# Feed-forward down projection of a two-layer decoder trunk: weight block B11 stays in SBUF for two block sums, every second f tile's four parts share one 8 KB buffer, and the low parts of u go to VectorE in the four products with a block sum

## The chip, the cores and the metric

The kernel runs on one core of a Trainium2 chip, as one program. The metric is the device time of one execution in microseconds (us), as the median of several runs.

## The reference

Two layers are applied to x[1, 1024, 1024] in float32. Layer 0 mixes tokens with forgetting attention and latent attention side by side, layer 1 with differential attention; behind each mixer stands a feed-forward part with a causal depthwise convolution. The change lies in the feed-forward part alone, in its last product.

```python
def _conv_ffn(h, w_up, conv_w, conv_b, w_down):
    gate, val = jnp.split(h @ w_up, [D_FF], axis=-1)          # D_FF = 2816
    act = jax.nn.gelu(_causal_dwconv(gate, conv_w, conv_b), approximate=True)
    return (act * val) @ w_down
...
    for layer in range(DEPTH):                                # DEPTH = 2
...
        x = x + _rms_norm(m, norm_mix_post[layer])
        h = _rms_norm(x, norm_ffn_pre[layer])
        f = _conv_ffn(h, ffn_w_up[layer], ffn_conv_w[layer], ffn_conv_b[layer], ffn_w_down[layer])
        x = x + _rms_norm(f, norm_ffn_post[layer])
```

## The kernel before

**Exact products from split operands.** TensorE (PE) multiplies float32r operands, which carry fewer bits than float32. So each operand is split: `split` (L120) copies the leading bits to `hi` on ScalarE (ACT, line L122 in the trace) and subtracts them from the raw value to get `lo` on the engine given to it (L123). A product is three matmuls: hi·hi, hi·lo and lo·hi (`hl`, `mm3`, L143).

**The down projection (`ffn_down`, once in each layer).** u = act · val is 1024 tokens x 2816 features, W_down 2816 x 1024. Both are cut into 2 x 2 blocks: u into A11 ... A22 (token half, f half), W_down into B11 ... B22 (f half, column half). Strassen's scheme in Winograd's form needs seven block products in place of eight, with sums of blocks as operands. Sums of u (S1 to S4) were made by the up projection and lie in DRAM (`u_d`, in the trace uS; plain blocks uA). Sums of weights are made here on VectorE (DVE) by `comb` (L675), f tile by f tile: T3 = B22 - B12, T2 = T3 + B11, T1 = B12 - B11, T4 = B21 - T2. T3 and then T2 stay in three 8 KB buffers `t3q` (dT in the trace), so that T4 can use T2.

The products run on PE strictly one after another: A11·B11, A12·B21, S3·T3, S2·T2, S1·T1, S4·B22, A22·T4. Each has 11 f tiles (NP = 11, taken in pairs by the loop over `g0`), and an f tile 4 token tiles x 3 = 12 matmuls of 128 x 512, so that a product has 132. Four PSUM banks hold a product's result, and products alternate between two sets of four (`sa`, `sb_`). Between products their results are added up in the tiles C (`q1`, `c11`, `q7`, `c22`), mostly on DVE. `fin_e` and `fin_a` start the norm of finished rows (`post_early`, L200 on POOL; `post_late`, L209 to L213), `fin_b` transposes the next layer's normed rows on PE (layer 0 only). The last product keeps its last 5 f tiles (`TAIL`) back and then does them token tile by token tile.

**What a pair of f tiles takes.** One SyncE (SP) load of u (`uraw`, two buffers of pool `raw`); a load of weights through `bload` (L669; `wdraw`, six 4 KB buffers of pool T) or, for a sum, two for T3 and T1 and one for T2 and T4, then `comb`; per f tile two `split` calls into four buffers `d` (ah, al, bh, bl) of 2 KB from pool Q, which has 18, that is room for four and a half f tiles. The lo parts of u go to GpSimd (POOL), those of the weights to DVE; only in the first pair of A11·B11 both go to POOL. B11 is loaded three times in a layer: for A11·B11, T2 and T1. The pool X has fourteen 8 KB buffers; here it holds dT (3), C (4), and the rows of the norm (`xq`).

**What sets the order.** The code gives the instructions in program order; the framework's scheduler then orders each engine's list by its own model of the durations, and pools hand out buffers in that order. At run time every engine takes its list strictly in order, waiting on semaphores. So the order is fixed at build time, and an instruction that waits holds up all that stand behind it on its engine. SP issues the loads in such a list too.

Of the kernel before, what the change touches and what calls it, by code (L numbers as in the profile page):

```python
# [14 lines left out]
AF = mybir.ActivationFunctionType  # L15
# [32 lines left out]
# columns of the packed per-partition vectors  # L48
C_CW = 0            # [layer][tap][f]
C_CB = 132          # [layer][f]  # L50
# [12 lines left out]
def trunk(ctx: ExitStack, tc: tile.TileContext, a: dict):  # L63
# [36 lines left out]
    # the table that has Sqrt, before there is anything to take a root of  # L100
    warm = sb.tile([P, 1], F32, tag="warm", name="warm")
    nc.scalar.activation(warm, epsc, AF.Sqrt)
    # the tensor engine's clock rises after some microseconds of work: products that nobody reads, while the
    # first loads are on their way
# [15 lines left out]
    def split(raw, hi, lo, lo_eng=nc.gpsimd):  # L120
        """hi + lo == raw exactly: hi keeps the leading bits that a float32r product takes, lo the rest"""
        nc.scalar.copy(R(hi), raw)  # L122
        lo_eng.tensor_tensor(R(lo), raw, hi, ALU.subtract)  # L123

    def wload(src, n, tag="WL", cw=HALF, lo_eng=nc.gpsimd):
        """n columns per partition of weights -> [(hi, lo)] in chunks of cw columns"""
# [27 lines left out]
    def rstd_col(ss, scale, which):  # L154
        """(ss * scale + eps) ** -0.5 of one column, refined once"""
# [8 lines left out]
    def rstd_newton(ss, scale, out, eps=None):  # L164
        """(ss * scale + eps) ** -0.5 without the Sqrt table: a seed from the exponent bits, three Newton steps"""
# [20 lines left out]
    def xq_pair(tag):  # L186
        """two [tok, d] tiles: the residual's rows, the normalised ones"""
# [8 lines left out]
    def post_early(n, src, g_post, junk):  # L196
        """for a column half that is there before the other: its squares' sum, then times the gain (in place)"""
# [5 lines left out]
    def post_late(m, n, src, sse, early, g_post, xi, xq, pool, cut=False):  # L203
        """x[xi + 1][m] = x[xi][m] + norm(rows) * g_post; column half n last, the other from post_early"""
# [12 lines left out]
    def pre_norm_a(xq, g):  # L217
        """xr [tok, d] -> normalised rows"""
# [6 lines left out]
    def pre_norm_b(xq, evac):  # L225
        """normalised rows, transposed; evac(kg, bank) takes [d in 4 tiles, tok]"""
# [20 lines left out]
    def hk(hT, half, k, ts=slice(0, HALF)):  # L247
        """(hi, lo) of feature tile k, a token half"""
        return tuple(hT[half, k // 4, j][:, k % 4, ts] for j in range(2))

    def projT(w, hT, half, nk=KT, M=P, tag="mm"):
        """(W^T h^T)[M, half of the tokens]; w: chunks of 4 feature tiles"""
# [9 lines left out]
    # Other products fill the tensor engine beside attention. They are generators that yield after a few  # L262
# [1059 lines left out]
```

## Time and profile before

| | us |
|---|---|
| median of three runs | 2642.51 (2638.03, 2642.51, 2645.48) |
| profiled execution, span | 2644.6 |
| its PE busy | 2482.9 (94%) |
| layer 0, the seven products | 1098.4 to 1339.0 |
| layer 1, the seven products | 2391.1 to 2632.8 |

For the profiled execution the trace gives its span, 2644.6 us, and no other time; the span is inside the spread of the three runs. Times in the trace are counted from the start of the span. A row of the timeline reads: start, duration, engine, line, operation, out<-in, shape, count of instructions grouped in the row, and in brackets the idle time of the engine ahead of it with what ended that idle time. A row of windows gives the stretch, its length, the busy time of PE, PEld (weight load), DVE, ACT and POOL with their instruction counts, then TensorE's granted clock (1.00 is 2.4 GHz, 0.50 is 1.2 GHz), the share of the DMA engines' time and GB/s. The down projection is 241 us of the span in layer 0 and 242 us in layer 1; the rest (attention, up projections) is not touched by the change.

### The profile page before, as it was taken

The page shows a single profiled execution, that of the slowest core. Times are in us where ns is not written, and L with a number is a line of the kernel's source. Part 1 is how long each engine was busy: PE and PEld are TensorE (multiplying, and loading weights), DVE is VectorE, ACT ScalarE, POOL GpSimd, SP SyncE. Part 2 cuts the span into 40 slices and gives each one's busy share as a digit, 9 for nine tenths or more (in the row PEclk, how much of TensorE's full clock was granted, in tenths as well). Part 3 has the DMA queues.
Part 4 walks back from the last instruction along what each step waited for, and adds up shares of the span by engine and source line. Part 5 has one row for each costly group of instructions (what it writes and reads, how often), then busy time and mean ns, then how long its engine had stood idle before and what let it go on. Part 6 is the DMA issues. An engine that isn't in the chain of part 4 may idle for free.

```text
span 2644.6 us, 36732 instructions
## 1 busy us (share of the span) xinstructions
PE 2482.9 (94%) x12326; PEld 2077.6 (79%) x12326; DVE 1831.6 (69%) x3539; ACT 1235.4 (47%) x2463; POOL 1451.3 (55%) x1264
## 2 busy tenths in 40 slices
PE   9999899997899999989989999999969999999897
PEld 7878788786688888777778888978757888887685
DVE  5555788658866676576876776776787656665758
ACT  4455578655333333344545555555443333334343
POOL 2445665436787767656521323232278776766575
PEclk9999999899899999999999999999989999999999
DMA  3332323334132222575531212133522232226764
GB/s 138 91 90 77 117 78 92 101 107 160 52 113 107 106 99 107 192 247 196 199 136 57 64 53 82 59 96 104 167 88 83 105 112 99 107 109 219 254 218 149
DMA packets 177597, 319.31 MB, mean 121 GB/s; under 512 B 17256, under 2 KB 68088, under 8 KB 177408
## 3 DMA queue, kind: packets, MB, share of 16 engines
q1 hardware_dynamic: 177408, 316.97, 35.9%
q8 instruction: 97, 1.59, 0.2%
q14 instruction: 92, 0.75, 0.1%
HBM read 225.37 MB, written 76.85 MB: 114 GB/s over the span
## 4 chain that ended last, share of the span: by engine, by line
PE 56%; DVE 13%; DMA 5%; issue 3%; POOL 2%; ACT 2%; SPq 0%; POOLq 0%; DVEq 0%; ACTq 0%
PE psmm L143 26%; PE pstr L143 10%; PE psS L143 9%; PE pspv L143 8%; DMA wdraw<-in_ffn_down_dram 3%; DVE d L123 2%; PE pstr L370 1%; DVE xn L223 1%; DVE wdraw L675 1%; POOL d L123 1%; DVE dT L675 1%; DMA uraw<-uA 1%; DVE t L339 1%; DVE xq L211 1%; PE pstr L1133 0%
## 5 line engine op out<-in xcount | busy, mean ns | idle before, releaser
L123 POOL TENSOR_TENSOR d<-uraw,d 128x512 fp32r<-128x512 f32 x154 | 237.5, 1559 | 150.2 <-ACT d L122 130.2
L143 PE MATMUL psmm<-hT,whi 128*128 128x512 f32 (+1 forms) x960 | 310.5, 400 | 0.3 <-DVE qb L311 0.3
L123 POOL TENSOR_TENSOR wlo<-wraw,whi 128x512 fp32r<-128x512 f32 (+2 forms) x96 | 128.4, 1345 | 261.0 <-ACT whi L122 249.5
L347 ACT ACTIVATE t<-t,mn 128x896 f32<-128x896 f32 (+7 forms) x256 | 198.9, 778 | 124.5 <-DVE mn L339 116.0
L143 PEld LDWEIGHTS psmm<-hT,whi 128*128 128x128 f32 (+1 forms) x960 | 175.5, 190 | 33.9 <-PE pstr L1152 0.4
L143 PE MATMUL psmm<-hT,wlo 128*128 128x512 f32 (+1 forms) x480 | 189.7, 396 | 0.0
L143 PE MATMUL psS<-d,d 128*128 128x512 f32 x528 | 149.9, 410 | 31.9 <-DVE d L123 23.2
L123 DVE TENSOR_TENSOR d<-wdraw,d 128x512 fp32r<-128x512 f32 x106 | 130.9, 1260 | 65.6 <-ACT d L122 58.7
L122 ACT CAST d<-uraw 128x512 fp32r<-128x512 f32 x154 | 95.0, 617 | 172.4 <-DMA uraw<-uS 73.0
L597 DVE TENSOR_TENSOR u<-u,psmm 128x512 f32<-128x512 f32 x44 | 30.2, 687 | 190.6 <-PE psmm L143 166.7
L143 PEld LDWEIGHTS psS<-d,d 128*128 128x128 f32 x528 | 100.2, 195 | 64.5 <-DVE d L123 33.8
L143 PE MATMUL psmm<-wo,ot 128*128 128x512 f32 x576 | 147.7, 397 | 0.0
L143 PE MATMUL pstr<-d,d 128*128 128x512 f32 x594 | 147.6, 392 | 0.0
L370 PE MATMUL pstr<-ident,t 128*128 128x128 f32 x864 | 136.7, 280 | 7.4 <-POOL t L887 1.7
L143 PE MATMUL psmm<-d,d 128*128 128x512 f32 x462 | 135.5, 396 | 6.5 <-DVE d L123 6.4
L143 PEld LDWEIGHTS pstr<-d,d 128*128 128x128 f32 x594 | 112.6, 190 | 23.9
L608 ACT ACTIVATE y<-y,cols 128x1024 f32<-128x1024 f32 x44 | 50.7, 1153 | 170.4 <-DVE y L606 170.4
L143 PE MATMUL psmm<-whi,hT 128*128 128x256 f32 (+1 forms) x576 | 123.4, 300 | 3.0 <-DVE qb L311 1.6
L143 PEld LDWEIGHTS psmm<-wo,ot 128*128 128x128 f32 x576 | 105.8, 189 | 20.8 <-DVE qb L311 0.2
L370 PEld LDWEIGHTS pstr<-ident,t 128*128 128x128 f32 x864 | 103.2, 145 | 16.7 <-POOL t L887 3.5
L375 DVE TENSOR_TENSOR ptq<-pstr,ptq 128x512 fp32r<-128x512 f32 (+1 forms) x160 | 99.4, 630 | 22.2 <-ACT ptq L374 18.1
L143 PE MATMUL psmm<-T,S2h 128*128 128x512 f32 x352 | 110.2, 393 | 4.8 <-DVE T L123 4.8
(342 smaller groups left out, 7491.5 us busy)
## 6 DMA issues: line engine op xcount, KB each, us to landing
wdraw<-in_ffn_down_dram SPq DMA_DIRECT2D x90, 512.0 KB, 4.9
wg<-in_ffn_up_dram SPq DMA_DIRECT2D x44, 512.0 KB, 3.4
wv<-in_ffn_up_dram SPq DMA_DIRECT2D x44, 512.0 KB, 3.4
uS<-us SPq DMA_DIRECT2D x88, 256.0 KB, 2.0
uraw<-uS SPq DMA_DIRECT2D x40, 512.0 KB, 4.8
uA<-y SPq DMA_DIRECT2D x66, 256.0 KB, 2.1
ot<-oT SPq DMA_DIRECT2D x64, 256.0 KB, 3.4
uraw<-uA SPq DMA_DIRECT2D x30, 512.0 KB, 4.1
```

The lines of the kernel that those rows point to most:

```text
L122: nc.scalar.copy(R(hi), raw)
L123: lo_eng.tensor_tensor(R(lo), raw, hi, ALU.subtract)
L143: ins = nc.tensor.matmul(out, R(l), R(r), start=first and j == 0, stop=last and j == n - 1).ins
L211: nc.vector.scalar_tensor_tensor(xn[:, cs], src, r, g_post[:, cs], ALU.mult, ALU.mult)
L223: nc.vector.scalar_tensor_tensor(xn, xr, r, g, ALU.mult, ALU.mult)
L339: nc.vector.tensor_tensor_reduce(t[:, d0:d1], sp[:, d0 - c0:d1 - c0], bb[:, d0:d1], scale, BIG if mn is None else mn, ALU.add, ALU.min, m2)
L347: nc.scalar.activation(t[:, :W], t[:, :W], AF.Exp, bias=mn, scale=-1.0, accum_out=l)
L370: nc.tensor.transpose(tp[:, c:c + P], pts[qi][:, b * P:(b + 1) * P], ident)
L375: nc.vector.tensor_tensor(R(pl[:, :c]), tp[:, :c], ph[:, :c], ALU.subtract)
L597: nc.vector.tensor_tensor(u2, s1, p6, ALU.add)
L608: nc.scalar.activation(y, y, AF.Gelu_apprx_tanh, bias=cb)
L675: nc.vector.tensor_tensor(d, xx, yy, op)
```

## The change

The diff also drops comments and docstrings, which moves line numbers; left out below. What it does, all in `ffn_down`:

- Three more X buffers, `b11q` (dB in the trace), take B11 directly from DRAM, in six loads per layer. A11·B11 splits from them, and `comb` for T2 and T1 reads them. The twelve loads of B11 for T2 and T1 in each layer are gone (54 weight loads per layer become 42), and B11 takes no T buffer.
- With `wide`, the second f tile of each pair has its four parts in one X buffer ([P, 4, 512], 8 KB) in place of four Q buffers. It is on in all products of layer 1 and in the first five of layer 0. The last f tile of the last product keeps its two T buffers.
- In the products with T1, T2, T3 and T4 the lo parts of u are subtracted on DVE and no longer on POOL: 44 instructions in each layer, 88 in all.
- One ACT instruction (`warm`, a square root of a constant column) stands at the head of `ffn_down`.

```diff
         wd = a["ffn_down"][layer]
-        t3q = [buf("X", "dT") for _ in range(3)]
+        b11q, t3q = ([buf("X", n) for _ in range(3)] for n in ("dB", "dT"))
         t3 = lambda g: t3q[g // 4][:, g % 4, :]
+        b11 = lambda g: b11q[g // 4][:, g % 4, :]
+
+        nc.scalar.activation(warm, epsc, AF.Sqrt)
...
         def btiles(name, g, n):
+            t, b0 = ([f(g + i) for i in range(n)] for f in (t3, b11))
+            if name == "B11":
+                nc.sync.dma_start(b11q[g // 4][:, g % 4:g % 4 + n, :], wd[g:g + n, :, :HALF].rearrange("g p c -> p g c"))
+                return b0
             if name[0] == "B":
                 return bload(int(name[1]) - 1, int(name[2]) - 1, g, n)
-            t = [t3(g + i) for i in range(n)]
             if name == "T1":
                 b = bload(0, 1, g, n)
-                return comb(b, b, bload(0, 0, g, n), ALU.subtract)
+                return comb(b, b, b0, ALU.subtract)
             if name == "T3":
                 return comb(t, bload(1, 1, g, n), bload(0, 1, g, n), ALU.subtract)
             if name == "T2":
-                return comb(t, t, bload(0, 0, g, n), ALU.add)
+                return comb(t, t, b0, ALU.add)
...
-        def prod(an, bn, tags, between=(), tail=0):
+        def prod(an, bn, tags, between=(), tail=0, wide=True):
...
                         ah, al, bh, bl = t = tuple(x[:, c * HALF:(c + 1) * HALF] for x in (buf("T", "d"), buf("T", "d")) for c in range(2))
+                    elif i and wide:
+                        dq = buf("X", "d")
+                        ah, al, bh, bl = t = tuple(dq[:, c, :] for c in range(4))
                     else:
                         ah, al, bh, bl = t = tuple(buf("Q", "d") for _ in range(4))
-                    split(ar[:, i * HALF:(i + 1) * HALF], ah, al, nc.gpsimd)
+                    split(ar[:, i * HALF:(i + 1) * HALF], ah, al, nc.vector if bn[0] == "T" else nc.gpsimd)
...
-        p = prod("S4", "B22", sb_)
+        p = prod("S4", "B22", sb_, wide=layer == 1)
...
-        p = prod("A22", "T4", sa, [lambda t=t: fin_b(t) for t in range(4)], TAIL)
+        p = prod("A22", "T4", sa, [lambda t=t: fin_b(t) for t in range(4)], TAIL, layer == 1)
```

Where the instructions now stand is shown at three places. First, DVE in layer 0 at the start of S3·T3. Before (L739 adds A12·B21's banks to C and so waits for that product's end on PE; `dT<-dT,wdraw` is T2's sum, `d<-dT,d` a lo part of the weights of S3·T3):

```order
L739 TENSOR_TENSOR C2686_11318<-C2685_11317,psmm2749_11576 128x512
L739 TENSOR_TENSOR C2686_11318<-C2685_11317,pstr2750_11577 128x512
L675 TENSOR_TENSOR dT2682_11314<-dT2682_11314,wdraw2888_12125 128x512 x2
L739 TENSOR_TENSOR C2686_11318<-C2685_11317,pstr2751_11578 128x512
L739 TENSOR_TENSOR C2686_11318<-C2685_11317,pstr2752_11579 128x512
L675 TENSOR_TENSOR dT2682_11314<-dT2682_11314,wdraw2898_12171 128x512
L123 TENSOR_TENSOR d2842_11927<-dT2682_11314,d2841_11926 128x512
L675 TENSOR_TENSOR dT2682_11314<-dT2682_11314,wdraw2898_12171 128x512
L123 TENSOR_TENSOR d2849_11955<-dT2683_11315,d2848_11954 128x512
L675 TENSOR_TENSOR dT2683_11315<-dT2683_11315,wdraw2908_12217 128x512
L123 TENSOR_TENSOR d2853_11975<-dT2683_11315,d2852_11974 128x512
L675 TENSOR_TENSOR dT2683_11315<-dT2683_11315,wdraw2908_12217 128x512
```

And in the changed kernel, the twelve rows that end with the lo parts of f tile 4 of S3·T3, `d2808` from u and `d2810` from T3 (`wdraw<-wdraw,dB` is T1's sum, for the product after next; x2 means two instructions; the first of the four L748, the old L739, stands fourteen rows above the first row here):

```order
L678 TENSOR_TENSOR dT2685_11317<-dT2685_11317,dB2682_11314 128x512
L678 TENSOR_TENSOR wdraw2893_12404<-wdraw2893_12404,dB2683_11315 128x512 x2
L678 TENSOR_TENSOR wdraw2900_12447<-wdraw2900_12447,dB2683_11315 128x512 x2
L678 TENSOR_TENSOR dT2685_11317<-dT2685_11317,dB2682_11314 128x512
L678 TENSOR_TENSOR wdraw2907_12490<-wdraw2907_12490,dB2684_11316 128x512 x2
L678 TENSOR_TENSOR dT2685_11317<-dT2685_11317,dB2682_11314 128x512
L678 TENSOR_TENSOR wdraw2914_12533<-wdraw2914_12533,dB2684_11316 128x512
L678 TENSOR_TENSOR dT2686_11318<-dT2686_11318,dB2683_11315 128x512
L123 TENSOR_TENSOR d2808_11915<-uraw2804_11906,d2807_11914 128x512
L123 TENSOR_TENSOR d2811_11934<-uraw2804_11906,d2811_11934 128x512
L123 TENSOR_TENSOR d2819_11979<-dT2686_11318,d2819_11979 128x512
L123 TENSOR_TENSOR d2810_11917<-dT2686_11318,d2809_11916 128x512
```

Between the first L748 and the lo parts of f tile 4 stand all of T1's sums, and lo parts of u, where before T2's sums and lo parts of the weights took turns.

Second, SP at the same place of layer 0. Before (L669 weights, L706 u; wdraw2888 to wdraw2938 are B11 for T2):

```order
L669 DMA wdraw2878_12092<-in_ffn_down_dram 128x512
L669 DMA wdraw2888_12125<-in_ffn_down_dram 128x2x512
L669 DMA wdraw2898_12171<-in_ffn_down_dram 128x2x512
L706 DMA uraw2843_11944<-uS30_107 128x2x512
L669 DMA wdraw2908_12217<-in_ffn_down_dram 128x2x512
L669 DMA wdraw2918_12263<-in_ffn_down_dram 128x2x512
L669 DMA wdraw2928_12309<-in_ffn_down_dram 128x2x512
L669 DMA wdraw2938_12355<-in_ffn_down_dram 128x512
L706 DMA uraw2854_11992<-uS30_107 128x2x512
L669 DMA wdraw2948_12392<-in_ffn_down_dram 128x2x512
```

In the changed kernel (L672 weights, L712 u; wdraw2879 to wdraw2914 are B12 for T1; uraw2804 is the third pair of S3·T3):

```order
L672 DMA wdraw2829_12043<-in_ffn_down_dram 128x512
L712 DMA uraw2796_11861<-uS30_107 128x2x512
L672 DMA wdraw2830_12045<-in_ffn_down_dram 128x512
L672 DMA wdraw2879_12318<-in_ffn_down_dram 128x2x512
L672 DMA wdraw2886_12361<-in_ffn_down_dram 128x2x512
L672 DMA wdraw2893_12404<-in_ffn_down_dram 128x2x512
L672 DMA wdraw2900_12447<-in_ffn_down_dram 128x2x512
L672 DMA wdraw2907_12490<-in_ffn_down_dram 128x2x512
L672 DMA wdraw2914_12533<-in_ffn_down_dram 128x512
L712 DMA uraw2804_11906<-uS30_107 128x2x512
```

The six loads ahead of a u load were T2's and are now T1's; they stand ahead of the third pair's u, where before they stood ahead of the fourth's (uraw2854).

Third, DVE in layer 1's last product, A22·T4. Before (L211 and L213 are the norm of rows that S4·B22 finished; `d<-wdraw,d` is a lo part of T4; the last of them is `d6151`):

```order
L213 SCALAR_TENSOR_TENSOR xq6083_25658<-C5687_24027,rrpost6086_25664,xq6083_25658 128x512
L211 SCALAR_TENSOR_TENSOR xq6088_25677<-C5686_24026,rrpost6091_25683,gains5682_24021 128x512
L213 SCALAR_TENSOR_TENSOR xq6088_25677<-C5687_24027,rrpost6091_25683,xq6088_25677 128x512
L161 SCALAR_TENSOR_TENSOR rrpost6096_25702<-cvpost6095_25701,rrpost6096_25702 128x1
L123 TENSOR_TENSOR d6131_25839<-wdraw6123_25812,d6130_25838 128x512
L123 TENSOR_TENSOR d6137_25865<-wdraw6133_25858,d6136_25864 128x512
L211 SCALAR_TENSOR_TENSOR xq6093_25696<-C5686_24026,rrpost6096_25702,gains5682_24021 128x512
L213 SCALAR_TENSOR_TENSOR xq6093_25696<-C5687_24027,rrpost6096_25702,xq6093_25696 128x512
L123 TENSOR_TENSOR d6141_25873<-wdraw6133_25858,d6140_25872 128x512
L123 TENSOR_TENSOR d6147_25887<-wdraw6143_25880,d6146_25886 128x512
L123 TENSOR_TENSOR d6155_25906<-wdraw6153_25902,d6155_25906 128x512
L123 TENSOR_TENSOR d6151_25895<-wdraw6143_25880,d6150_25894 128x512
```

In the changed kernel (`d5945` is the product's last lo part):

```order
L123 TENSOR_TENSOR d5944_25673<-uraw5942_25668,d5944_25673 128x512
L160 SCALAR_TENSOR_TENSOR cvpost5890_25446<-rrpost5891_25447,cvpost5890_25446 128x1
L159 RECIPROCAL rrpost5901_25485<-cspost5902_25486 128x1
L160 SCALAR_TENSOR_TENSOR cvpost5895_25465<-rrpost5896_25466,cvpost5895_25465 128x1
L161 SCALAR_TENSOR_TENSOR rrpost5886_25428<-cvpost5885_25427,rrpost5886_25428 128x1
L123 TENSOR_TENSOR d5945_25674<-wdraw5943_25670,d5945_25674 128x512
L161 SCALAR_TENSOR_TENSOR rrpost5891_25447<-cvpost5890_25446,rrpost5891_25447 128x1
L160 SCALAR_TENSOR_TENSOR cvpost5900_25484<-rrpost5901_25485,cvpost5900_25484 128x1
L161 SCALAR_TENSOR_TENSOR rrpost5896_25466<-cvpost5895_25465,rrpost5896_25466 128x1
L211 SCALAR_TENSOR_TENSOR xq5883_25422<-C5599_23929,rrpost5886_25428,gains5592_23920 128x512
L213 SCALAR_TENSOR_TENSOR xq5883_25422<-C5600_23930,rrpost5886_25428,xq5883_25422 128x512
L211 SCALAR_TENSOR_TENSOR xq5888_25441<-C5599_23929,rrpost5891_25447,gains5592_23920 128x512
```

All lo parts of the product now stand ahead of the four pairs of L211 and L213, which before stood among them.

## Rows read from the trace of the kernel before

**Rows 1.** The page's first part: busy time, share and instructions of each engine.

```profile
PE 2482.9 (94%) x12326; PEld 2077.6 (79%) x12326; DVE 1831.6 (69%) x3539; ACT 1235.4 (47%) x2463; POOL 1451.3 (55%) x1264
```

**Rows 2.** Windows of layer 0's products, without the sixth (columns as told above).

```profile
1098.40:1131.90 33.50, 31.41 (x133) 24.50 (x134) 21.26 (x15) 14.07 (x25) 27.81 (x18) 1.00 0.78 274
1131.90:1163.30 31.40, 30.20 (x133) 24.59 (x132) 18.51 (x19) 14.31 (x26) 16.80 (x12) 1.00 0.74 250
1163.30:1204.60 41.30, 33.73 (x134) 26.33 (x133) 35.07 (x35) 14.61 (x30) 24.07 (x16) 0.92 0.70 248
1204.60:1235.80 31.20, 30.22 (x134) 24.64 (x133) 16.11 (x18) 15.92 (x29) 19.12 (x13) 1.00 0.53 179
1235.80:1265.70 29.90, 29.90 (x133) 24.76 (x132) 19.53 (x19) 13.34 (x24) 22.71 (x15) 1.00 0.58 200
...
1296.00:1339.00 43.00, 36.55 (x159) 28.22 (x158) 40.33 (x85) 25.27 (x56) 16.44 (x10) 0.96 0.46 157
```

**Rows 3.** Windows of layer 1's products, without the fifth and sixth.

```profile
2391.10:2427.80 36.70, 34.58 (x132) 26.70 (x133) 20.91 (x15) 14.10 (x25) 27.68 (x18) 0.91 0.74 251
2427.80:2459.30 31.50, 30.35 (x134) 24.73 (x133) 18.90 (x19) 14.31 (x26) 16.89 (x12) 1.00 0.73 248
2459.30:2499.60 40.30, 33.75 (x133) 25.17 (x132) 33.46 (x35) 13.68 (x29) 22.31 (x15) 0.96 0.70 251
2499.60:2535.10 35.50, 32.40 (x133) 25.75 (x133) 16.65 (x19) 16.91 (x31) 20.43 (x15) 0.95 0.50 161
...
2595.00:2632.80 37.80, 32.27 (x133) 25.49 (x131) 32.88 (x58) 16.07 (x37) 22.62 (x14) 0.95 0.28 94
```

**Rows 4.** Timeline of PE where it waits in the products.

```profile
1098.37 0.73 PE L143 MATMUL psS<-d,d 128*128 128x512 f32 x2 [1.33 <-ACT d L122]
...
1179.15 2.50 PE L143 MATMUL psS<-d,d 128*128 128x512 f32 x5 [5.03 <-DVE d L123]
...
1324.48 1.09 PE L231 MATMUL pstr<-ident,xq 128*128 128x128 f32 x8 [0.73 <-DVE xq L223]
...
2511.84 0.86 PE L143 MATMUL psmm<-d,d 128*128 128x512 f32 x2 [2.20 <-DVE d L123]
...
2614.75 2.50 PE L143 MATMUL psS<-d,d 128*128 128x512 f32 x5 [4.08 <-DVE d L123]
```

**Rows 5.** Timeline of SP: two waits ahead of weight loads in layer 0.

```profile
1087.92 15.51 SPq L669 DMA_DIRECT2D wdraw<-in_ffn_down_dram  x3
...
1174.55 12.42 SPq L669 DMA_DIRECT2D wdraw<-in_ffn_down_dram  x3
```

**Rows 6.** Timeline of POOL: the last two dT buffers (pool X) of layer 0 are written.

```profile
1083.73 0.33 POOL L734 MEMSET dT<- 128x1 f32 x2 [1.13 <-PE pstr L143]
```

**Rows 7.** Timeline of DVE: the same kind of instruction, alone and beside POOL.

```profile
1175.64 1.78 DVE L675 TENSOR_TENSOR dT<-dT,wdraw 128x512 f32<-128x512 f32 x1
...
1264.92 0.68 DVE L751 TENSOR_TENSOR C<-C,psS 128x512 f32<-128x512 f32 x1
1265.52 0.67 DVE L750 TENSOR_TENSOR C<-C,psS 128x512 f32<-128x512 f32 x1
```

**Rows 8.** Timeline of POOL beside them.

```profile
1180.20 5.10 POOL L123 TENSOR_TENSOR d<-uraw,d 128x512 fp32r<-128x512 f32 x3
```

**Rows 9.** Line L123 by engine: count, ns min/median/max, first and last start.

```profile
L123 POOL TENSOR_TENSOR d<-uraw,d x154: 1259/1726/2266, 1081.3 to 2622.2; 128x512 fp32r<-128x512 f32 x154
```

**Rows 10.** Timeline of DVE in layer 1's S2·T2.

```profile
2510.49 0.69 DVE L675 TENSOR_TENSOR wdraw<-wdraw,wdraw 128x512 f32<-128x512 f32 x1 [3.92 <-DMA wdraw<-in_ffn_down_dram]
```

**Rows 11.** Timeline of DVE in layer 0's A22·T4: the last lo part.

```profile
1328.85 0.68 DVE L123 TENSOR_TENSOR d<-wdraw,d 128x512 fp32r<-128x512 f32 x1
```

**Rows 12.** Timeline of DVE in layer 1's A22·T4.

```profile
2611.20 1.75 DVE L213 SCALAR_TENSOR_TENSOR xq<-C,rrpost,xq 128x512 f32<-128x512 f32 x1
2612.88 1.21 DVE L161 SCALAR_TENSOR_TENSOR rrpost<-cvpost,rrpost 128x1 f32<-128x1 f32 x1
...
2622.02 2.47 DVE L123 TENSOR_TENSOR d<-wdraw,d 128x512 fp32r<-128x512 f32 x2 [0.93 <-ACT d L122]
```

## The prediction, as put on record before the changed kernel ran

> **What bounds the kernel now.** I read the page's busy times first: PE is busy 94% of the span, DVE, the next engine, 69% [rows 1]. So time can be gained only where PE waits or runs at half clock, and the change lies in the two down projections. Next I cut the windows at the first matmul of each product [rows 2, 3]. The fifth product of layer 0, S1·T1, takes 29.9 us with PE busy all through at clock 1.00: that is 132 matmuls x 0.2265 us, and what a product costs when nothing is late. Every product's excess over 29.9 is therefore the most that the change can take from it. Layer 0: A11·B11 3.6, A12·B21 1.5, S3·T3 11.4, S2·T2 1.3, S4·B22 0.4 (it lies between the rows shown, 1265.7 to 1296.0), A22·T4 13.1, of which some 3 are 24 transposes that stand inside it (eight take 1.09 [rows 4]). Layer 1: 6.8, 1.6, 10.4, 5.6, then nothing, then 7.9. In all about 31 + 32 - 3 = 60 us, and 1.3 us ahead of each first product (the first row of [rows 4]).
>
> Then who is late. The timeline of PE [rows 4] names DVE's lo parts at the three large waits: 5.03 us in S3·T3, 2.20 in S2·T2, 4.08 in A22·T4. After such waits the granted clock of the window is 0.92 to 0.96, where PE was idle before: part of each excess is matmuls at half clock. DVE is busy 35.07 of 41.30 us in S3·T3, and POOL 24.07 [rows 2]. The same 128 x 512 subtraction or sum takes 0.68 us alone with 0.60 between starts, and 1.78 beside a POOL operation [rows 7]; POOL's own lo part is 1.70 there (5.10 / 3, [rows 8]) and 1.26 at best [rows 9]. So DVE is slow in S3·T3 because POOL works beside it, and it is late because of that. In two places it is a load instead: DVE waits 3.92 us for a weight load in S2·T2 [rows 10], and SP stands before a weight load for 12.42 us in S3·T3 and for 15.51 us ahead of the first product, until a T buffer is free [rows 5].
>
> **The change, part by part.** (1) *Moving 88 lo parts to DVE.* In the four T products of a layer POOL gives up 44 x 1.26 to 1.73 us [rows 9], 55 to 76 us, and DVE takes 44 x 0.60 = 26 us. For one product that is 11 x 0.60 = 6.6 us more on DVE. S1·T1 and S2·T2 have room for it (DVE 16 to 20 of 30 us, and that with POOL beside it), so nothing is charged there: the cover is PE's 29.9 us, and it would be gone only if DVE exceeded it. Two operations shared between the engines take about 1.75 us together, two on DVE alone 1.2: moving is a gain for the pair, as long as DVE has room.
>
> The Trainium skill has a rule that speaks against it: "Perfetto Trace Analysis", Optimizing Scalar/DVE Operations, says that a saturated DVE is a reason to give work to other engines. "SBUF — State Buffer", Who interferes with whom, says that an operation of DVE that reads two SBUF operands and one of GpSimd exclude each other on a shared port. The trace agrees with the second (0.68 against 1.78). By the first, S3·T3 with its DVE at 85% should get worse; that is the slower rival below.
>
> (2) *A11·B11.* The B11 loads go to X buffers, not to T buffers, so the 15.51 us of SP's wait [rows 5] is shortened; X buffers come free about 4 us ahead of the first T buffer (the dT buffers of that pool are written by 1084.1 [rows 6], the wdraw load issues at 1087.92). But in the changed order casts and lo parts that wait for loads stand ahead of the up projection's last Gelu steps, which free the product's banks, so some stall stays. Bounds: nothing, and the whole excess with the wait ahead (3.6 + 1.3, 6.8 + 1.3). I take half and a little more: -2.3 in layer 0, -5 in layer 1 (there the wide buffers also help the 0.91 clock).
>
> (3) *A12·B21.* Here PE waits once, at one late tile; eight and a half tiles of look-ahead in place of four and a half take all of it: -1.5 and -1.6.
>
> (4) *S3·T3.* Both ends are far apart. The order now has, from the first L748 (which waits for A12·B21's last matmul, so it cannot run before about the product's start) to `d2810`, the last lo part that f tile 4 needs, 31 instructions on DVE (26 rows, five of them x2). At 0.60 that is 18.6 us; with one or two of them started earlier 16.8, and with four of POOL's gain multiplications beside (each slows one DVE instruction by 1.1) 21.2. PE needs tile 4 after 4 x 2.7 = 10.8 us. So it waits 6 to 10.4 us, and then runs some 1.7 to 3.4 us longer at half clock, as after the 5.03 us wait of before. That makes 29.9 + 7.7 to 13.8 = 37.6 to 43.7 us against 41.3 and 40.3. The loads say the same: the third pair's u is queued on SP behind six loads of T1 (2.9 MB; at the 248 GB/s of this window 11.6 us). So this product, the largest excess, keeps its stall, for another reason. Middle: -0.6 and +0.4; I take +0.5 and +1, since it also starts earlier against its loads. Bounds -3.6 to +3.4 each.
>
> (5) *S2·T2.* No load of B11, and T2 is summed before the product: the excess goes whole, -1.3 and -5.6. S1·T1 and S4·B22: 0 and -0.3.
>
> (6) *A22·T4, layer 1.* The last lo part ends at 2624.5, 29.5 us after the product's start [rows 3, 12], behind the norms' L211 and L213, of which one takes 1.75 us and a step of one column 1.21, because POOL's lo parts run beside. Now all lo parts stand ahead of the norms. From the first L764 (the old L755) to the last lo part there are 16 large instructions, 9.6 us at 0.60, and some 16 of one column; with a wait for ACT between and up to three slowed ones 13 to 15 us. PE keeps 5 tiles back and needs the last after 7 x 2.7 = 19 us. The excess of 7.9 goes but for a little: -7.6, bounds -8 and -4. The norms shift behind it; their cover is the 13 us of PE behind tile 6, and if that is short the end after PE (11.8 us, 2644.6 - 2632.8) grows; 2 us at the most.
>
> (7) *A22·T4, layer 0.* Here it isn't wide, but POOL is off DVE: the last lo part came 33.5 us after the product's start [rows 2, 11] and comes now at about 25 to 29, since the lo parts of u and of T4, 22 in all, go at 0.60 and not in pairs of 1.75; and fewer of the transposes stand in the way. Of the 10.4 us excess I take -3, bounds 0 and -7.
>
> (8) *`warm`.* The order has both copies at the very start of the program, right behind the old one: nothing.
>
> Sum, layer 0: -2.3 - 1.5 + 0.5 - 1.3 - 0.3 - 3 = -7.9. Layer 1: -5 - 1.6 + 1 - 5.6 - 7.6 = -18.8. In all -26.7 against the profiled execution, 2644.6 - 26.7 = 2617.9; the median of before lies 2.1 under that span, so I state 2642.5 - 26.7 = 2616 us.
>
> **The rivals.** *More is gained.* If S3·T3's stall is only the 248 GB/s of loads, and these run ahead (T1's loads can start while T3's end), PE waits 2 to 3 us less there than I take, or not at all; with A11·B11 clean (-4.9, -8.1) and layer 0's tail at -7, the sum is -26.7 - 5.7 - 4 - 2 x 3 = about -42: 2600 us. For it: DVE's 35 busy us hold at least ten instructions slowed from 0.68 to 1.78. Against: the 31 instructions in one row. 0.22.
>
> *The gain goes elsewhere.* X has 14 buffers; dB, dT and C hold ten, so the wide tiles live on four, and gains and `xq` want some too. If the wide tiles wait for a buffer, (2), (3) and (5) shrink to nothing, and (6) to half: -26.7 + 7.3 + 3.1 + 6.9 + 3.8 = about -6: 2637 us. For it: SP's long waits of before were all for buffers. 0.11.
>
> *Slower.* One mechanism: DVE's list at the start of S3·T3. It is saturated there by the order, and each instruction that stalls in it (for T1's loads, which six of them read) holds all lo parts behind it. Price: it has to grow S3·T3 by 13.5 us in each layer over what I take to eat the gain, and by 17.5 to be slower by over 0.3%. That is PE waiting 20 us and more for tile 4, which takes T1's six loads (11.6 us) to begin only after L748 and to be followed by the third pair's u and the 15 instructions left. It would give about 2652 us. 0.06. That `warm` does nothing is in all of these. The rule of the Trainium skill on a saturated DVE, named above, would give this rival's time.
>
> **How the numbers follow.** The forecast's own case has 0.61, the rivals 0.22, 0.11 and 0.06. Within 0.3%, 7.9 us, is about what a measurement of this kernel can tell from no change: faster is below 2634.6. The second rival is partly there; faster 0.83, same 0.11, slower 0.06. The likeliest case has four terms with wide bounds: (2) -5.7 and +7.3 about what I took, (4) -8.7 and +5.3, (6) -0.4 and +3.6, (7) -4 and +3. Taken as independent (the root of the sum of squares) that is -11 and +10: 2605 to 2626. To hold eight in ten the range goes down into the first rival and up to the edge of the second: 2599 to 2633.
>
> **What will show it.** PE in S2·T2 of layer 1 at 29.9, in A12·B21 at 29.9, in A22·T4 of layer 1 near 30. A wait of 6 to 10 us of PE near 11 us into S3·T3, put down to a lo part on DVE, with T1's sums ahead of it. DVE's large instructions at 0.68 and not 1.78 in S1·T1. If S3·T3 is at 30 to 33, the first rival was right; over 45, the last; if PE waits for casts or lo parts in A12·B21 with X buffers late, the second. I would be wrong altogether if attention, whose code and order are as before, moved by more than 2 us.

## The result, and the profile after

The changed kernel takes 2619.93 us (median of four runs, 2619.34 to 2623.52) against 2640.58 us (four runs, 2638.03 to 2645.48): a ratio of 0.9916, 95% interval 0.9904 to 0.9928. That is 20.7 us faster. Forecast were 2616 us and a range of 2599 to 2633. The profiled execution has a span of 2621.7 us, 22.9 under the 2644.6 of before; forecast was -26.7.

First the page's busy times, which answer to [rows 1], in the same columns:

```profile
PE 2469.2 (94%) x12326; PEld 2074.5 (79%) x12326; DVE 1813.6 (69%) x3627; ACT 1235.6 (47%) x2465; POOL 1311.3 (50%) x1176
```

DVE has 88 instructions more (3627 against 3539) and is busy 18 us less; POOL has 88 less and is busy 140 us less. The windows by product show where. The changed kernel, layer 0's seven products, then layer 1's; [rows 2, 3] answer to them:

```profile
1095.20:1125.10 29.90, 29.90 (x133) 24.71 (x132) 17.79 (x18) 11.15 (x19) 17.96 (x16) 1.00 0.76 247
1125.10:1159.80 34.70, 31.85 (x134) 25.86 (x133) 21.51 (x26) 14.20 (x27) 12.46 (x9) 0.95 0.82 290
1159.80:1200.80 41.00, 32.50 (x133) 26.10 (x132) 32.95 (x50) 14.56 (x31) 6.41 (x4) 0.88 0.31 108
1200.80:1230.80 30.00, 30.00 (x134) 24.82 (x134) 20.12 (x34) 19.00 (x36) 0.00 (x0) 1.00 0.61 198
1230.80:1260.70 29.90, 29.90 (x134) 24.75 (x133) 14.51 (x19) 7.93 (x16) 11.40 (x9) 1.00 0.44 141
1260.70:1290.60 29.90, 29.90 (x133) 24.76 (x132) 22.96 (x28) 14.39 (x28) 16.46 (x11) 1.00 0.61 215
1290.60:1322.80 32.20, 31.85 (x145) 25.66 (x143) 29.05 (x77) 21.02 (x45) 2.53 (x2) 1.00 0.47 160
```

```profile
2377.90:2408.50 30.60, 30.30 (x134) 24.75 (x134) 17.50 (x18) 11.25 (x19) 17.62 (x16) 1.00 0.71 241
2408.50:2440.00 31.50, 30.17 (x133) 24.66 (x132) 19.80 (x22) 11.08 (x21) 12.56 (x9) 1.00 0.80 285
2440.00:2483.80 43.80, 33.58 (x133) 26.25 (x132) 35.34 (x53) 17.51 (x36) 7.94 (x4) 0.88 0.37 125
2483.80:2513.70 29.90, 29.90 (x133) 24.77 (x132) 20.21 (x33) 19.13 (x37) 0.00 (x0) 1.00 0.62 201
...
2543.60:2576.50 32.90, 30.54 (x133) 24.62 (x133) 25.90 (x29) 12.95 (x26) 17.27 (x11) 1.00 0.64 227
2576.50:2606.70 30.20, 30.17 (x133) 24.51 (x131) 27.71 (x61) 14.46 (x34) 8.45 (x5) 1.00 0.62 202
```

Six of the fourteen products now stand at the bound of 29.9 to 30.0 us, two more within 0.7 of it (three of the six, S1·T1 of both layers and S4·B22 of layer 0, were there or within 0.4 before). What is left is S3·T3 in both layers (41.0 and 43.8), A12·B21 (34.7, before 31.4, and 31.5 as before in layer 1), S4·B22 of layer 1 (32.9, before 30.0) and A22·T4 of layer 0 (32.2). Against before, layer 0's seven products take 13.0 us less, layer 1's 12.9, the first of them starts 3.2 earlier, the stretch between the two layers' products is 3.0 longer and the end behind PE's last one 3.2 longer: -22.9 in all. In the last product of layer 0 DVE is busy 29.05 us, before 40.33. PE's timeline at the three largest waits:

```profile
1139.91 0.73 PE L143 MATMUL psmm<-d,d 128*128 128x512 f32 x2 [2.85 <-DVE d L123]
...
1180.51 2.08 PE L143 MATMUL psS<-d,d 128*128 128x512 f32 x4 [8.00 <-DVE d L123]
...
2463.07 2.07 PE L143 MATMUL psS<-d,d 128*128 128x512 f32 x4 [8.40 <-DVE d L123]
```

The two waits of 8 us, which end 20.7 and 23.1 us into S3·T3, are the forecast's wait for f tile 4. DVE's timeline ahead of the first of them (L678 with `wdraw<-wdraw,dB` is T1's sum, with `dT<-dT,dB` T2's; L123 are lo parts):

```profile
1168.45 2.38 DVE L678 TENSOR_TENSOR wdraw<-wdraw,dB 128x512 f32<-128x512 f32 x2
1170.75 0.68 DVE L123 TENSOR_TENSOR d<-dT,d 128x512 fp32r<-128x512 f32 x1
1171.36 0.68 DVE L678 TENSOR_TENSOR dT<-dT,dB 128x512 f32<-128x512 f32 x1
1171.96 2.48 DVE L678 TENSOR_TENSOR wdraw<-wdraw,dB 128x512 f32<-128x512 f32 x4
1174.37 0.68 DVE L678 TENSOR_TENSOR dT<-dT,dB 128x512 f32<-128x512 f32 x1
1174.97 1.28 DVE L678 TENSOR_TENSOR wdraw<-wdraw,dB 128x512 f32<-128x512 f32 x2
1176.17 0.68 DVE L678 TENSOR_TENSOR dT<-dT,dB 128x512 f32<-128x512 f32 x1
1176.78 0.68 DVE L678 TENSOR_TENSOR wdraw<-wdraw,dB 128x512 f32<-128x512 f32 x1
1177.38 0.68 DVE L678 TENSOR_TENSOR dT<-dT,dB 128x512 f32<-128x512 f32 x1
1177.98 1.28 DVE L123 TENSOR_TENSOR d<-uraw,d 128x512 fp32r<-128x512 f32 x2
1179.18 1.27 DVE L123 TENSOR_TENSOR d<-dT,d 128x512 fp32r<-128x512 f32 x2
```

And ACT's, which casts that tile's u:

```profile
1168.05 1.12 ACT L122 CAST d<-uraw 128x512 fp32r<-128x512 f32 x2
```

The load of u had landed and was cast by 1169.2. Its lo part came at 1177.98, behind nine sums of T1, four of T2 and a lo part of T3, with no idle time between them. So here the load isn't late, DVE's list is.

### The profile page after: what moved, and what is told of

Its sections match the earlier page's. It is cut to its first block, busy times and chain, and to the rows that moved or that the text cites. A ratio compares the mean times of both kernels' runs of the same rounds, so it can differ in the third digit from the quotient of the medians.

```text
span 2621.7 us, 36473 instructions
## 1 busy us (share of the span) xinstructions
PE 2469.2 (94%) x12326; PEld 2074.5 (79%) x12326; DVE 1813.6 (69%) x3627; ACT 1235.6 (47%) x2465; POOL 1311.3 (50%) x1176
## 5 line engine op out<-in xcount | busy, mean ns | idle before, releaser
L123 POOL TENSOR_TENSOR wlo<-wraw,whi 128x512 fp32r<-128x512 f32 (+2 forms) x96 | 126.4, 1325 | 293.8 <-ACT whi L122 250.6
L597 DVE TENSOR_TENSOR u<-u,psmm 128x512 f32<-128x512 f32 x44 | 30.2, 687 | 181.8 <-PE psmm L143 163.6
L123 POOL TENSOR_TENSOR d<-uraw,d 128x512 fp32r<-128x512 f32 x66 | 99.1, 1518 | 86.2 <-ACT d L122 86.1
L123 DVE TENSOR_TENSOR d<-wdraw,d 128x512 fp32r<-128x512 f32 x88 | 83.9, 976 | 47.2 <-ACT d L122 46.3
L143 PE MATMUL psmm<-B,A11h 128*128 128x512 f32 x352 | 110.6, 393 | 3.1 <-ACT B L500 3.1
L143 PE MATMUL psS<-B,S4h 128*128 128x512 f32 x352 | 110.6, 396 | 2.8 <-ACT S4h L122 2.8
L143 PE MATMUL psmm<-B,A12h 128*128 128x512 f32 x352 | 111.2, 389 | 0.0
L143 PE MATMUL pstr<-T,S3h 128*128 128x512 f32 x352 | 111.1, 397 | 0.0
L143 PE MATMUL pstr<-T,A22h 128*128 128x512 f32 x352 | 109.4, 390 | 0.9 <-DVE T L123 0.9
```

What stands on the lines that cost most here:

```text
L143: ins = nc.tensor.matmul(out, R(l), R(r), start=first and j == 0, stop=last and j == n - 1).ins
L597: nc.vector.tensor_tensor(u2, s1, p6, ALU.add)
```

## The experiments

The time between the start of a product and the start of the next is called its length below. All kernels were timed beside the kernel before on the same chip; ratios are against those runs. Lengths of single products agree between executions far better than the span: the changed kernel and `u_warm`, which have the same order, differ by at most 1.1 us in any product, but by 3.9 us in when the first of them starts.

**The parts undone one at a time.** `u_lo`: lo parts of u back on POOL.

```diff
-split(ar[...], ah, al, nc.vector if bn[0] == "T" else nc.gpsimd)
+split(ar[...], ah, al, nc.gpsimd)
```

> The changed kernel with the lo parts of u back on GpSimd in the four products with a block sum; B11 kept and the wide buffers stay. Theory (the parts add, and VectorE's lists beside GpSimd set the tails): both last products A22·T4 lose their gain again (7.6 us in layer 1, 8 to 10 in layer 0), S2·T2 stays at 29.9 us and the first products stay short; so 15 to 20 us above the changed kernel, about 2635 to 2640. Rival (fewer loads and more buffers do everything, the engine of the lo parts is indifferent): within 4 us of the changed kernel, 2616 to 2624.

Measured: 2646.97 us, ratio 1.0017 (1.0008 to 1.0026). All of the gain is gone, and a little more: 27 us above the changed kernel, where the theory had 15 to 20. A22·T4 is at 42.7 and 38.5 us again, and S3·T3, which the theory had not charged, at 48.6 and 47.8. In layer 0's S3·T3, PE's wait at f tile 4 became:

```profile
1187.75 2.08 PE L143 MATMUL psS<-d,d 128*128 128x512 f32 x4 [14.62 <-DVE d L123]
```

The window of that product:

```profile
1158.80:1207.40 48.60, 32.24 (x134) 25.55 (x133) 36.36 (x38) 15.96 (x33) 27.86 (x17) 0.86 0.29 102
```

T1's sums stand in the same place there, now beside POOL's lo parts. Two of DVE's rows:

```profile
1169.98 3.48 DVE L678 TENSOR_TENSOR wdraw<-wdraw,dB 128x512 f32<-128x512 f32 x2
...
1177.92 3.42 DVE L678 TENSOR_TENSOR wdraw<-wdraw,dB 128x512 f32<-128x512 f32 x2
```

That is 1.7 us for a sum, where it is 0.6 from start to start alone. The rival (the engine doesn't matter) falls.

`u_keep`: B11 loaded again for T2 and T1, into T buffers, where A11·B11 gets its own too; the buffers dB are gone.

```diff
...
-return comb(b, b, b0, ALU.subtract)                  # T1
+return comb(b, b, bload(0, 0, g, n), ALU.subtract)
...
-return comb(t, t, b0, ALU.add)                       # T2
+return comb(t, t, bload(0, 0, g, n), ALU.add)
```

> The changed kernel with B11 loaded again for each of its two block sums, through the T buffers as before; lo parts on VectorE and the wide buffers (now with three more X buffers free) stay. Theory: S2·T2 of layer 1 and the first products get their waits for weight loads back, +5.6 and +6 to +10 us, the last products stay short: 2630 to 2637. Rival (the lo parts are the whole gain): within 4 us of the changed kernel.

Measured: 2623.49 us, ratio 0.9929 (0.9913 to 0.9946), which is the rival's number: B11 in SBUF is worth 0 to 4 us here. By product it gives and takes. A11·B11 is 32.7 us in both layers against 29.9 and 30.6, A12·B21 37.7 and 38.8, but S3·T3 only 34.2 and 32.4, where T1's first sum comes 18.7 us into the product and no longer ahead of f tile 4's lo parts. And S2·T2 is at the bound although B11 is loaded again:

```profile
1202.30:1232.30 30.00, 30.00 (x133) 24.67 (x132) 22.36 (x37) 18.14 (x35) 0.00 (x0) 1.00 0.57 186
2487.20:2517.10 29.90, 29.90 (x134) 24.75 (x133) 22.79 (x38) 18.30 (x35) 0.00 (x0) 1.00 0.69 220
```

`u_wide`: all parts in Q buffers.

```diff
-elif i and wide:
+elif False:
```

> The changed kernel with every f tile's parts in four Q buffers again, four and a half tiles of look-ahead; B11 kept and lo parts on VectorE stay. Theory: look-ahead smooths A11·B11 and A12·B21 only, so +3 to +8 us: 2623 to 2628. Rival (look-ahead is what carries the long lists of VectorE, without it the lo parts come late in every product): +15 us and more, 2635 and above.

Measured: 2618.59 us, ratio 0.9913 (0.9898 to 0.9928): no difference from the changed kernel; both expectations were too high. A12·B21 is 31.0 and 29.9 us without the wide buffers, 34.7 and 31.5 with them, and S4·B22 of layer 1 29.9 without and 32.9 with them; A22·T4 of layer 1 is 35.8 without and 30.2 with them. Layer 0's A12·B21 and layer 1's A22·T4 in `u_wide`:

```profile
1125.70:1156.70 31.00, 30.40 (x133) 24.58 (x133) 17.21 (x20) 13.19 (x25) 13.76 (x10) 1.00 0.77 250
2565.80:2601.60 35.80, 31.94 (x133) 25.67 (x131) 31.30 (x67) 16.63 (x39) 8.54 (x5) 0.95 0.33 112
```

**Parts alone.** `a_lo` is the kernel before with the lo parts moved and nothing else but the square root at the head of `ffn_down` (it is `u_keep` and `u_wide` together).

> The kernel before with one part of the change alone: the lo parts of u on VectorE in the four products with a block sum. B11 is loaded three times, all parts in Q buffers. Theory (the moved lo parts carry nearly the whole gain, also in S2·T2, since GpSimd no longer slows VectorE): about 2620 to 2626, A22·T4 of layer 1 at 30 to 36 us, S2·T2 at 29.9. Rival (it needs B11 in SBUF, else the weight loads hold S2·T2 of layer 1 at 35 us and the first products at 33 and 36 us): 2630 to 2636.

Measured: 2621.93 us, ratio 0.9924 (0.9908 to 0.9941), the same as the whole change within its interval. Layer 1's S2·T2, then its A22·T4:

```profile
2482.10:2512.00 29.90, 29.90 (x133) 24.77 (x132) 18.02 (x30) 14.75 (x27) 0.00 (x0) 1.00 0.55 174
2571.90:2606.10 34.20, 31.75 (x133) 25.57 (x131) 29.93 (x66) 15.72 (x37) 8.64 (x5) 0.95 0.33 113
```

`a_keep` is the kernel before with B11 kept and nothing else but that square root (`u_lo` and `u_wide` together).

> The kernel before with one part alone: B11 kept in SBUF for the block sums; lo parts of u on GpSimd, all parts in Q buffers. Theory (it shortens the first products and S2·T2, and lengthens S3·T3, whose list on VectorE takes T1's sums, slowed by GpSimd): first products -6 to -10 us, S2·T2 -7, S3·T3 +7 each, so about no change: 2636 to 2646. Rival (fewer loads are a gain by themselves): 2625 to 2630.

Measured: 2631.7 us, ratio 0.9956 (0.9942 to 0.9971), 10.7 us faster, between the two expectations. A11·B11 is at 29.9 in both layers, S2·T2 too, S3·T3 at 45.7 and 44.9, 4.4 and 4.6 us longer than before. With `u_lo` beside it the wide buffers can be priced: added to `a_keep` they cost 15 us, with the lo parts on DVE 2 to 3, which is about what medians of the same kernel differ by. So the parts don't add. In a table (us under the kernel before, from the medians of the same call; the changed kernel from its own):

| | narrow, B11 reloaded | narrow, B11 kept | wide, B11 reloaded | wide, B11 kept |
|---|---|---|---|---|
| lo parts on POOL | 0 | -10.7 | not run | +4.6 |
| lo parts on DVE | -20.5 | -23.8 | -18.9 | -20.7 |

`u_warm` leaves out the square root at the head of `ffn_down`; its order is that of the changed kernel but for one row at the program's start.

> The changed kernel without the square root of a constant at the head of the down projection. Its instructions stand in the same order on every engine but for that one row at the program's start. Theory: no change, 2618 to 2623, which also shows how far two builds of one order differ. Rival (it saves a load of ScalarE's tables at the norm): 1 to 3 us above the changed kernel per layer, 2622 to 2626.

Measured: 2620.78 us, ratio 0.9926 (0.9901 to 0.9952): nothing, as expected.

**What holds S3·T3.** `m1`: T1's sums are queued behind S3·T3's last lo part, the rest is left to the scheduler.

```diff
...
+with tc.issue_after(los["S3"][-1].ins):              # queue order only; los: the lo parts of each product's weights
-    return comb(b, b, b0, ALU.subtract)
+    return comb(b, b, b0, ALU.subtract)
```

> The changed kernel with one thing moved: T1's sums stand behind the last lo part of S3·T3 in VectorE's list, and no longer ahead of the lo parts of its f tile 4. Theory (the 8.0 and 8.4 us waits in S3·T3 are VectorE's queue: 11 sums of 0.60 us and what slows beside them): the wait at f tile 4 shrinks from 8 us to 0 to 2 in each layer, S3·T3 from 41.1 and 43.8 us to 30 to 35, together -14 to -22 us: 2598 to 2606. Rival (the third pair of u lands late behind T1's six loads): S3·T3 stays at 38 us or more, less than 6 us gained in all: 2614 to 2620.

Measured: 2607.25 us, ratio 0.987 (0.9856 to 0.9885). S3·T3 went from 41.0 to 31.8 and from 43.8 to 35.5 us, 17.5 us in all, of which about 12 show in the time (the stretch between the two layers' products, which the edit doesn't touch, was 1058.8 us and not 1055.1). PE's wait at layer 0's f tile 4, 8.00 before:

```profile
1173.93 1.20 PE L143 MATMUL psS<-d,d 128*128 128x512 f32 x4 [1.58 <-DVE d L123]
```

In layer 1 it is 3.37 us, 8.40 before. The theory holds, though layer 1's wait and the time (1 us) lie beyond what it gave: most of the wait was DVE's queue. T1's six loads still stand ahead of u on SP in `m1`, so they were not it.

**What holds A12·B21.** The trace of the changed kernel has it on ACT. Its timeline in layer 0 at the end of A11·B11, which is at 1125.3 (L745 copies that product's result), and then SP's next loads:

```profile
1123.33 0.59 ACT L745 COPY C<-psS 128x512 f32<-128x512 f32 x1 [5.63 <-PE psS L143]
1123.81 0.62 ACT L122 CAST d<-uraw 128x512 fp32r<-128x512 f32 x1
```

```profile
1126.39 0.38 SPq L672 DMA_DIRECT2D wdraw<-in_ffn_down_dram  x1
1126.82 0.47 SPq L712 DMA_DIRECT2D uraw<-uA  x1
```

The copy waits 5.63 us for PE with five casts of A12·B21 behind it. SP's last weight load ahead of those two was issued at 1117.2; that the loads wait for buffers which these casts free is read from the order of the rows. `m12` is `m1` with the four copies queued behind the casts of the first seven f tiles of A12·B21 (the expectation counts nine; the edit names the ninth cast from the end, which is the seventh tile's):

```diff
...
-for t in range(4):
-    nc.scalar.copy(q1[:, t, :], p[t])
 p = prod("A12", "B21", sb_)
+with tc.issue_after(casts[-9].ins):
+    for t in range(4):
+        nc.scalar.copy(q1[:, t, :], p1[t])           # p1: the banks of A11·B11
```

> As m1 (T1's sums behind S3·T3's lo parts), and ScalarE's four copies of A11·B11's result moved behind the casts of A12·B21's first nine f tiles. Theory (in A12·B21 the first copy, which waits for A11·B11's end, holds up casts behind it and so the loads into the buffers that they free): the 3 us wait in A12·B21 goes, 34.9 to 30 us in layer 0 and 31.5 to 30 in layer 1, 5 to 6 us under m1: 2601 to 2603. Rival (the wait is of the loads): same as m1, 2605 to 2609.

Measured: 2602.91 us, ratio 0.9845 (0.983 to 0.986). A12·B21 is at 29.9 us in both layers, here layer 0's:

```profile
1126.90:1156.80 29.90, 29.90 (x133) 24.76 (x132) 13.90 (x17) 10.93 (x21) 7.44 (x5) 1.00 0.81 287
```

S3·T3 of layer 0 took 3 us of it back (35.0): PE now waits 3.13 us at f tile 1. DVE had idled 2.12 us for a weight load just ahead of the product, which would fit a product that starts earlier against its loads; that was not tried.

`m5`: as `m1`, wide buffers only in layer 1's A22·T4.

> As m1, and with wide buffers in one product only, A22·T4 of layer 1. Theory (longer look-ahead does nothing but in that last product, where it keeps 30 us against 35.8; elsewhere it costs the waits of A12·B21 and S4·B22): A12·B21 30 to 31, S4·B22 29.9, the rest as m1: 7 to 9 us under m1, 2598 to 2601. Rival (without it S3·T3 and A11·B11 get waits of their own): 2604 to 2612.

Measured: 2606.82 us, ratio 0.9863 (0.9848 to 0.9877), the same as `m1`: the theory fell and the rival's number came. A12·B21 was 31.7 and 31.1 us, near the 30 to 31 it gave, but S4·B22 of layer 1 stayed at 32.5, and S3·T3 of layer 0 rose from 31.8 to 34.9. So S4·B22's loss isn't that of its own wide buffers. Those of the product behind it remain: with lo parts of S4·B22 on POOL, S4·B22 of layer 1 is 32.5 to 32.9 in all seven kernels whose A22·T4 of layer 1 is wide and 29.9 to 30.0 in the four where it isn't. By what way is not shown, since DVE makes 10 or 11 of T4's sums during S4·B22 with and without them.

**The rest of POOL's lo parts.** `m4`: as `m12`, and the lo parts of u on DVE in all products but the first.

```diff
-split(ar[...], ah, al, nc.vector if bn[0] == "T" else nc.gpsimd)
+split(ar[...], ah, al, nc.gpsimd if an == "A11" else nc.vector)
```

> As m12, and the lo parts of u on VectorE in all products but A11·B11, so in A12·B21 and S4·B22 too. Theory (VectorE alone at 0.60 us is quicker than both engines beside each other; in S4·B22 of layer 1 its list is slow because of GpSimd): S4·B22 of layer 1 from 32.8 to 30 us, A12·B21 stays at 29.9: 2599 to 2601. Rival (a saturated VectorE: the 22 more lo parts per layer come late, in A12·B21 above all, where it also makes T3's sums): A12·B21 at 32 us or more, 2604 to 2612.

Measured: 2589.05 us, ratio 0.9798 (0.9779 to 0.9817), 12 to 14 us under `m12` and 10 better than the theory. Windows of layer 0's A12·B21 and S3·T3, then of layer 1's S3·T3 and S4·B22:

```profile
1125.10:1155.00 29.90, 29.90 (x134) 24.77 (x132) 17.77 (x29) 12.67 (x24) 0.00 (x0) 1.00 0.85 299
1155.00:1185.30 30.30, 30.21 (x133) 24.71 (x132) 30.30 (x46) 13.75 (x29) 5.96 (x4) 1.00 0.39 133
2422.40:2452.30 29.90, 29.90 (x133) 24.78 (x132) 29.90 (x46) 13.17 (x27) 5.77 (x4) 1.00 0.37 124
2512.20:2542.70 30.50, 30.18 (x133) 24.67 (x132) 25.78 (x40) 13.83 (x28) 5.50 (x4) 1.00 0.75 268
```

DVE is busy all through S3·T3 (30.30 of 30.30 us) and PE no longer waits for it. The theory had charged nothing for S3·T3. Its first lo parts are made during A12·B21, where POOL is now idle: in layer 0 the first three of T3 end 7.4 and 1.6 us ahead of the product's start and 2.6 behind it, in `m12` 3.2 ahead, 2.7 and 6.9 behind it. That they are ready sooner for this reason fits, but wasn't tried apart.

`m8`: as `m4`, with T2's sums of a pair behind the lo part five f tiles further on.

> As m4, and T2's sums of a pair of f tiles stand behind the lo part of S3·T3's weights five f tiles further on. Theory (in S3·T3 of m12 the waits at f tile 1, 7.7 and 7.1 us with the tile itself, are VectorE's list, in which T2's sums stand between lo parts): S3·T3 from 35.0 and 34.3 to 31 to 33 us, 3 to 6 us under m4: 2594 to 2598. Rival (the wait is of T3's weight loads): same as m4.

Measured: 2589.43 us, ratio 0.9803 (0.9783 to 0.9823): the same as `m4`, since there was no wait left to take.

`x_allv`: the changed kernel with `m4`'s one line and nothing reordered.

> The changed kernel with the lo parts of u on VectorE in all products but A11·B11, and nothing reordered: T1's sums and the four copies stay where the changed kernel has them. Theory (two causes that add: queue order, and GpSimd slowing VectorE): from the first L748 to the last lo part of f tile 4 there are still 28 instructions, 16.8 us at 0.60, so S3·T3 keeps a wait of 4 to 7 us at f tile 4 in each layer and A12·B21 of layer 0 its 3 us; S4·B22 goes to 30 us: 2604 to 2612. Rival (GpSimd beside VectorE was the whole cause, also of those waits, and reordering is needless): 2589 to 2594, as m4.

Measured: 2612.26 us, ratio 0.9879 (0.9863 to 0.9896). S3·T3 stays at 39.9 and 41.3 us, with this wait at layer 0's f tile 4:

```profile
1176.62 1.65 PE L143 MATMUL psS<-d,d 128*128 128x512 f32 x3 [6.65 <-DVE d L123]
```

So there are two causes: the order of the lists (20 to 23 us between `x_allv` and `m4`, T1's sums on DVE and the copies on ACT together) and POOL beside DVE (12 to 14 between `m12` and `m4`). Of the theory one piece failed: A12·B21 of layer 0 was at 29.9 with the copies in place. DVE without POOL beside it seems quick enough to make good what the copies cost.

## Why the prediction was right, and where only its sum was

The sum was 4 us off in the span, -26.7 against -22.9; single terms were off by up to 8 one way and 5 the other.

- *(1) Lo parts on DVE, (6) A22·T4 of layer 1.* Right. 37.8 to 30.2 us, -7.6 as forecast, and `u_lo` puts it back to 38.5. But the moved lo parts alone don't do it: without the wide buffers the product takes 34.2 (`a_lo`) and 35.8 us (`u_wide`). There all four pairs of the norms' L211 and L213 stand ahead of the last eight lo parts, of which the last ends 25.4 and 26.8 us into the product; in the changed kernel it ends at 16.1. So the order that the forecast read off takes both parts. And the cover named for the norms behind it was short by more than the 2 us allowed: from PE's end to the span's end it is 15.0 us now (2621.7 - 2606.7), before 11.8. The add of the first token tile, which PE finished near 2596.5, stands behind the last norm of the rows before it on DVE:

```profile
2600.65 0.74 DVE L213 SCALAR_TENSOR_TENSOR xq<-C,rrpost,xq 128x512 f32<-128x512 f32 x1
2601.31 0.67 DVE L768 TENSOR_TENSOR C<-C,psS 128x512 f32<-128x512 f32 x1
```

That the order is the cause of these 3 us was not tried by itself.

- *(2) A11·B11.* Right in kind, sized too small: -3.6 and -6.1 us for the product alone, to the bound, against -2.3 and -5 with the wait ahead. `a_keep` has it at 29.9 in both layers with B11 kept alone, `a_lo` at 33.8 and 34.6 without. The casts ahead of the last Gelu steps cost nothing that shows. The two rows of [rows 5] were misread: each shows three loads, of which the first row holds one wait, of 14.2 us, and the second two, of 5.9 and 5.4, not waits of 15.51 and 12.42; no term rests on these figures.
- *(3) A12·B21.* Wrong: +3.3 and about 0 where -1.5 and -1.6 were forecast. The step that failed was that a longer look-ahead takes the wait away. With it, the casts for tiles further ahead are queued on ACT behind a copy that waits for PE's end of the product before (`m12`); without the wide buffers the product was 31.0 and 29.9 (`u_wide`). A wait for lo parts in A12·B21 was to be a sign of the second rival, but its losses in A11·B11 and S2·T2 did not come.
- *(4) S3·T3.* Right in its mechanism: DVE's list with T1's sums, PE waiting 8.0 and 8.4 us where 6 to 10.4 were given; -0.3 and +3.5 us for the product where +0.5 and +1 were taken and -3.6 to +3.4 bounded, the second just outside. The matmuls at half clock behind the wait (granted clock 0.88 in both windows; their starts are 0.43 us apart and not 0.23) cost 2.2 and 2.6 us (1.7 to 3.4 were given; 2.6 behind the 5.03 us wait of before). The second support, that u's load is late behind T1's loads, was wrong: it was cast 9 us before DVE came to it.
- *(5) S2·T2.* The size was right, -1.2 and -5.6, the reason too narrow. The reload of B11 wasn't needed for the wait: with the lo parts moved it is at the bound with reloads (`u_keep`, `a_lo`), and with B11 kept it is there with the lo parts on POOL (`a_keep`). Either part is enough, so neither part's undoing shows it. S4·B22 of layer 1, forecast at 0, lost 2.9 us: it comes with the wide buffers of the product behind it (`m5`), and with its own lo parts moved off POOL too it went to 30.5 (`m4`).
- *(7) A22·T4 of layer 0.* Too small: 43.0 to 32.2, -10.8, where -3 was taken and -7 was the bound. Part was given back behind the product, where transposes now stand that were inside it (145 PE instructions in the window against 159): from its end to layer 1's first product it is 1055.1 us, before 1052.1. Over all kernels run, that stretch is 1053.7 to 1059.3 us in the eleven whose A22·T4 of layer 0 takes 34 us or less, and 1047.9 to 1052.1 in the three where it takes 42 to 43. The means are 1056.5 and 1050.1, so some 6 us come back and the net is about -4, near the -3 taken. The fourteen transposes are 1.9 us of that (eight take 1.09); what the rest is was not tried.
- *(8)* Right (`u_warm`).
- *The rivals.* The slower one, a DVE saturated in S3·T3, was nearer than its 0.06: with POOL still beside DVE (`u_lo`) half of its price came, S3·T3 some 7 us longer in each layer than before and than forecast (13.5 were to eat the gain), and that took back 14.8 of the 16.7 us that A11·B11 and S2·T2 gained there. The Trainium skill's rule on a saturated DVE ("Perfetto Trace Analysis", Optimizing Scalar/DVE Operations), that giving some of its work to ScalarE or even GpSimd may make sense, speaks for leaving the lo parts on POOL. Here the runs speak against it: in layer 0's S3·T3 DVE is busy 36.36 us with 38 instructions in `u_lo` and 32.95 us with 50 in the changed kernel, and the product is 7.6 us shorter. The same section of the Trainium skill adds that the two engines share an SBUF read port, so that moving work between them might not help. The traces agree so far that a DVE operation takes longer beside POOL (1.7 us and not 0.6); the port itself is in no row.
- *The sign of being wrong altogether* (attention moving by more than 2 us) came by its number: the first product starts 3.2 us earlier, and the stretch between the layers is 3.0 longer. It was set too tight: in `u_warm`, with the changed kernel's order, that start differs by 3.9.

The forecast's mechanisms held in the main but for (3); that its sum came within 4 us was luck, since errors of both signs cancelled. Against the terms 17 us were lost (A12·B21 6.4, S3·T3 1.7, S4·B22 2.9, behind layer 0's last product 3.0, at the end 3.2) and 13 made up (A22·T4 of layer 0 7.8, A11·B11 2.4, and a first product that began 3.2 us earlier). That last is within the 3.9 us by which that start differs between two kernels of one order.

## What to carry to other kernels

Where two engines slow each other, look at the sum of their work: giving POOL's part to DVE made DVE's own busy time shorter with more instructions in its list. Then read the list of the busy engine at the product that waits: work that nobody needs yet (here T1's sums, two products early) is put there because its inputs are ready, and moving it back by order alone was worth 12 us, with the copies on ACT another 4 to 7. Test parts of a change alone and undone: here one line carried most of the gain, one part was worth 11 us alone and 2 to 3 beside that line, and one cost 15 us without the line and with it 2 to 3, which can't be told from nothing.

## What the runs showed that was not expected

A saturated DVE with POOL nearly off it (four instructions, 5.96 us) feeds PE without a wait: 46 instructions, 30.30 of 30.30 us busy, S3·T3 at 30.3 us. The fastest kernel of the study, `m4` (`m8` can't be told from it), has both layers' seven products at 213.1 and 210.8 us, against 240.6 and 241.7 before and a floor of 209.3 (7 x 29.9).
